# Feed-forward gate and up: high weights times both parts of x as one matmul of 512 columns, the halves added on the way out of PSUM

## The chip, the cores and the metric

The kernel runs on one core of one Trainium2 chip. The metric is the device time of one execution in microseconds; the median over the runs shown is used. Engines are named as in the profile: PE (TensorE's matmuls) and PEld (its weight loads), DVE (VectorE), ACT (ScalarE), POOL (GpSimd), SP (SyncE, which issues the DMAs).

## What is computed

A stack of four layers on one sequence of 256 tokens with 1024 features, in float32: two mixers with adaptive norms (sparse attention, dilated attention), and then two layers that each have a mixer (latent with sliding-window attention; forgetting with chunked attention) and a feed-forward part, each closed by a layer norm. The change touches the two feed-forward parts:

```python
def _swiglu(x, w_gate, w_up, w_down):
    g = jnp.einsum('bsd,df->bsf', x, w_gate)
    u = jnp.einsum('bsd,df->bsf', x, w_up)
    return jnp.einsum('bsf,fd->bsd', jax.nn.silu(g) * u, w_down)

    for layer in range(DEPTH):
        ...
        x = _layer_norm(DEEPNORM_ALPHA * x + mix, ln1_g[layer], ln1_b[layer])
        ffn = _swiglu(x, w_gate, w_up, w_down)
        x = _layer_norm(DEEPNORM_ALPHA * x + ffn, ln2_g[layer], ln2_b[layer])
```

Gate and up are 1024 x 2816, down is 2816 x 1024.

## The kernel before

Every float32 matrix product is made of three products of a narrower type (float32r). An operand is split exactly into a high part (rounded on ACT) and a low part (the rest, subtracted on DVE), and high x high, high x low and low x high are added up in PSUM. For activations `to_T` does this: four transposes on PE, a cast on ACT (L292), a subtraction on DVE (L293). The transposed operands of all 256 tokens stand in two tiles, `xh` and `xl`, of 8 chunks of 128 features by 256 tokens; `xt_tiles` gives the strips of 128 tokens of one block.

Weights are streamed in the order of use as units of 1024 floats per partition (512 KB). `make` loads a unit by DMA (L205), casts it on ACT (L210) and subtracts on DVE (L211). At most `NB` = 8 units stand ready or in use; `get` takes units, and `done`, called as the last products that use a unit are issued, lets the next one be made (`pump`). The new unit's cast waits until the slot that it takes over has been read.

`dense_T` computes 512 columns of x @ W, transposed: columns on the partitions, all 256 tokens along the free axis. It takes 4 units. For each pair of blocks of 128 columns it fills one PSUM bank, block after block, 256 floats each: 8 chunks of three products of 256 columns (L277 high weights with xh, L278 high weights with xl, L279 low weights with xh). Then the pair's sink is called. `dense_cols` is the other form, tokens on the partitions.

The feed-forward part (`ffn`) goes over the hidden features in six groups, the first of 256 columns (with `dense_cols`), five of 512 (with `dense_T`). For each group it computes gate, then up, then the products of the group before it with the down weights (`down`, L239, L240, L243 through `products`, 512 columns each). `gate_sink` makes a tanh on ACT (L472) and a product on DVE (L473); `up_sink` multiplies on DVE (L1035) and splits the hidden features by a cast on ACT (L1039) and a subtraction on DVE (L1040). PSUM banks go round by kind: four for the sums of `down`, three (4, 5, 6) of kind `gu` for gate and up, one for transposes.

The order of each engine's queue is fixed before the run by a scheduler that goes by dependences between parts of tiles, by its own model of time, and by priority; a sink stands 300 instructions ahead of its place in the program (`first(SINK)`). It is not written out by hand, so any edit may shift it.

Of the kernel before, what the change touches and what calls it, by code (L numbers as in the profile page):

```python
# [21 lines left out]
# priority, in instructions, that work of a kind has over what was emitted before it  # L22
SINK, HEAD, ATTN = 300, 60, 1200
# weights: floats of a unit per partition, units loaded ahead, units split ahead
UNIT, RAW, NB = 1024, 5, 8
# eighths of adaLN's rows loaded ahead
# [68 lines left out]
def body(ctx: ExitStack, tc: tile.TileContext, A: dict, out: bass.AP, stop=None):  # L95
# [17 lines left out]
    # ---- PSUM banks: each kind of tile goes round its own banks  # L113
# [12 lines left out]
    # ---- constants  # L126
# [52 lines left out]
    # ---- weights: streamed in order, split exactly into two float32r parts  # L179
# [6 lines left out]
    def spec(W, k0, nk, cols):  # L186
        """nk chunks of 128 rows of W from chunk k0 on, of the given ranges of columns side by side"""
        specs.append((W, k0, nk, cols))
# [42 lines left out]
    def products(p, terms, c, start=True, stop=True, after=None):  # L231
        """p += the products of chunks (xt, k) with (weights, kw): of the high parts of several chunks
        with both parts of the weights first, as the low parts come last"""
        n = len(terms)
        for t0 in range(0, n, state["group"]):
            group = range(t0, min(t0 + state["group"], n))
            for t in group:
                xt, k, w, kw = terms[t]
                pe.matmul(p, lhsT=xt[0][:, k, :], rhs=w[0][:, kw, c], start=start and t == 0, stop=False)  # L239
                pe.matmul(p, lhsT=xt[0][:, k, :], rhs=w[1][:, kw, c], start=False, stop=False)  # L240
            for t in group:
                xt, k, w, kw = terms[t]
                pe.matmul(p, lhsT=xt[1][:, k, :], rhs=w[0][:, kw, c], start=False, stop=stop and t == n - 1)  # L243
                if after is not None:
                    after(t)

    def dense_cols(xts, nk, n, sink, kind="mm"):
        """a group of n columns of x @ W, block of tokens after block of tokens; the sink takes them from PSUM"""
        step = UNIT // n
        units = -(-nk // step)  # L250
        ws = get(units)
        for tok in range(2):
            p = ps(kind)[:, :n]
            products(p, [(xts[tok], k, ws[k // step], k % step) for k in range(nk)], slice(0, n),
                     after=lambda k: tok and (k % step == step - 1 or k == nk - 1) and done(1))
            with first(SINK):
                sink(tok, p)

    # ---- transposed operands
    xh = ap_.tile([128, 8, 256], F32R, name="xh")  # L260
    xl = ap_.tile([128, 8, 256], F32R, name="xl")

    def xt_tiles(tok):
        """the operands of a block of tokens: one after the other they go over the same memory"""
        return tuple(t[:, :, tok * 128:(tok + 1) * 128] for t in (xh, xl))

    def dense_T(n, sink, kind="mm"):
        """n columns of x @ W, transposed: two blocks of 128 columns after the other, of all tokens"""
        ws = get(4)
        for pair in range(n // 256):  # L270
            p = ps(kind)
            for c in range(2):
                cols = slice(pair * 256 + c * 128, pair * 256 + c * 128 + 128)
                o = p[:, c * 256:(c + 1) * 256]
                for k in range(8):
                    w = [part[:, k % 2, cols] for part in ws[k // 2]]
                    pe.matmul(o, lhsT=w[0], rhs=xh[:, k, :], start=k == 0, stop=False)  # L277
                    pe.matmul(o, lhsT=w[0], rhs=xl[:, k, :], start=False, stop=False)  # L278
                    pe.matmul(o, lhsT=w[1], rhs=xh[:, k, :], start=False, stop=k == 7)  # L279
                    if pair == n // 256 - 1 and c and k % 2:  # L280
                        done(1)
            with first(SINK):
                sink(pair, p)

    def to_T(src, n, xt, k0):
        """n blocks of 128 columns, transposed and split, to chunks k0.. of xt"""
# [9 lines left out]
    def transposes(dst, srcs, eng, width=128):  # L296
        """up to four [128, width] blocks, transposed to dst [width, n, 128]"""
# [12 lines left out]
    # ---- norms  # L310
# [14 lines left out]
    def deepnorm(layer, which, last=False):  # L325
        """the sink of a product that closes a sublayer: x <- LN(alpha x + p) * g + b, and its transposed parts"""
# [28 lines left out]
    def gated(tok, h, p, g, tp):  # L355
        """x += p * g"""
# [16 lines left out]
    def project_out(xts, sink, order):  # L373
        """the products of the four chunks that come first, and then those of the others, that close a block of
        tokens before the next, so that a norm runs beside products; none but those of the norms' operands
        are split beside the last"""
# [14 lines left out]
    # ---- rotations  # L391
# [3 lines left out]
    def rope(dst, src, H, hd, cos, sin, tp):  # L395
        """dst = rotated src; src [128, H, 2*hd], dst the same or with copies side by side"""
# [13 lines left out]
    # ---- attention of a head: scores of both blocks of queries side by side, [128 | 256 keys]  # L410
    BLOCKS = ((0, 128), (128, 384))

    def scores(qT, kT, masks=None):
        """masks(tok): (lhsT, rhs, c0, c1) added on the tensor engine"""
# [8 lines left out]
    def shifted(s, added, n2, tp, scale=1.0):  # L423
        """-scale * (s + added), and its least value of each block of queries"""
# [11 lines left out]
    def av(e, v, o, c0, start, eng, tp, stop=True):  # L436
        """o[tok][:, c0:c0+64] += e of the block times v(block of keys)"""
# [12 lines left out]
    # of the keys of both blocks for the second block's queries; the first block's are the last 128  # L450
# [9 lines left out]
    def close_heads(o, den, oxt, k0, tp):  # L460
        """eight heads' sums over their denominators, transposed"""
# [7 lines left out]
    def silu2(p, dst, tp):  # L469
        """dst = 2 silu(p)"""  # L470
# [4 lines left out]
    # ---- the order of the weights  # L475
# [45 lines left out]
    # ---- adaLN  # L521
# [9 lines left out]
    def ada_rows(rows, new, ahead):  # L531
        """rows (name, layer, column): 1024 columns of silu(c) @ w + b on every partition;
        that of the scale: (1 + that) * the norm's gain. Returns the function that does the next eighth
        of a row, behind an instruction, and loads what is wanted some steps on"""
# [46 lines left out]
    # =====================================================================  # L581
    # layer 0: native sparse attention
# [17 lines left out]
    # the first columns of the mixer, chunk by chunk of the features, as adaLN gives them  # L600
# [64 lines left out]
    # nothing before the loads that the products wait for  # L665
# [11 lines left out]
    # the operands of the compression: [2 tokens of a block, features] by 16 pairs of tokens  # L677
# [4 lines left out]
    with first(ATTN):  # L682
        pool.tensor_copy(cmask, cc[:, C_CADD:C_CADD + 2 * NCMP].rearrange("p (t n) -> p t n", t=2))
        for tok in range(2):
# [6 lines left out]
            # the lower half one token on  # L691
# [14 lines left out]
    def k_side(p, tok, a, b, i):  # L706
        """rotated keys of both groups, twice side by side, transposed"""
# [13 lines left out]
    with first(SINK):  # L721
# [9 lines left out]
        # with the half that the gated z, twice a silu, asks for  # L731
# [23 lines left out]
    # keys: those of a group twice, block-diagonal, for a pair of heads at once  # L755
# [9 lines left out]
    # values: block-diagonal over the eight heads of a group  # L765
# [14 lines left out]
    def cmp_probs(tok, g):  # L780
# [11 lines left out]
        if tok == 0:  # L792
            # the first queries see no compressed key at all
# [16 lines left out]
    def nsa_head(g, hh, o):  # L810
        """selected blocks (all that there are) and window: both causal over all keys"""
# [77 lines left out]
    # =====================================================================  # L889
    # layer 1: dilated attention  # L890
    assign(mm=[0, 1], s=[2, 3], pt=[4, 5], o=[6, 7])
    with tc.tile_pool(name="dil", bufs=1) as dp:
# [42 lines left out]
        with first(ATTN):  # L935
# [4 lines left out]
            # the patterns' weights: softmax of logsumexp - log(heads), with 3 for the patterns  # L940
            # and the half that the gated z asks for; the gates of the second heads with all their factors
# [50 lines left out]
    # =====================================================================  # L992
    def ffn(layer, xt, last):
        state["group"] = 2
        assign(d=[0, 1, 2, 3], gu=[4, 5, 6], pt=[7])
        with tc.tile_pool(name=f"ffn{layer}", bufs=1) as fp:
# [3 lines left out]
            def down(parts, sink=None):  # L1000
                """parts of the hidden features into the sums, block of tokens after block of tokens"""
# [19 lines left out]
            for g, (a, b) in enumerate(ffn_groups):  # L1021
# [4 lines left out]

                def gate_sink(i, p):
                    m = p.shape[1]
# [3 lines left out]
                def up_sink(i, p):  # L1032
                    m = p.shape[1]
# [8 lines left out]
                if g:  # L1042
                    dense_T(n, gate_sink, "gu")
                    dense_T(n, up_sink, "gu")
# [14 lines left out]
    # =====================================================================  # L1059
    # layer 2: latent attention + sliding window  # L1060
    assign(mm=[0, 1], s=[2, 3], pt=[4, 5], o=[6, 7])
    state["group"] = 1
    with tc.tile_pool(name="ab", bufs=1) as bp:
# [30 lines left out]
        def qs_sink(pair, p):  # L1094
            # over the slopes, that come back with the distances
# [73 lines left out]
    # =====================================================================  # L1169
    # layer 3: forgetting attention + chunked attention with relative positions  # L1170
    assign(mm=[0, 1], s=[2, 3], pt=[4, 5], o=[6, 7])
    state["group"] = 1
    with tc.tile_pool(name="cd", bufs=1) as dp:
# [7 lines left out]
        # queries and keys with two more features that add the decays: (q, 1, cum q) . (k, -cum k, 1)  # L1181
# [17 lines left out]
        def fvf_sink(tok, p):  # L1199
            act.activation(fv[:, tok, 256:512], p[:, :256], AF.Copy)  # L1200
            # min(f, 0) - log(1 + exp(-|f|))
# [30 lines left out]
        with first(ATTN):  # L1232
# [8 lines left out]
            for h in range(8):  # L1241
                hs = slice((h % 2) * 64, (h % 2) * 64 + 64)
                # rel[q - k + 63] for the second block's queries, keys in reverse; the first block's are its last 128
# [23 lines left out]
def arrange(inputs):  # L1267
# [10 lines left out]
    # by head, and led by the 64 distances that the mask covers  # L1278
# [20 lines left out]
```

## Time and profile before

| | |
|---|---|
| runs (us) | 1024.37, 1039.41, 1026.41 |
| median (us) | 1026.41 |
| profiled execution: span from first to last instruction (us) | 1024.7 |
| profiled execution: its own time | not given |
| PE busy (us) | 978.7 |
| DVE busy (us) | 662.3 |
| ACT busy (us) | 508.4 |
| mean granted clock of TensorE | 0.980 |
| moved by DMA | 177.75 MB |

The profile is of one execution. Busy time of an engine is the union of its instructions. Matmuls are pipelined, so durations of neighbours overlap, and the pace is read from the starts. In brackets behind an instruction stand the idle time of its engine just before it and what ended that.

### The profile page before, as it was taken

Reading aid. Unit: us, or ns where it says so; the run is one execution under the profiler, and the core shown is the slowest. Engines: PE = TensorE matmul, PEld = TensorE weight load, DVE = VectorE, ACT = ScalarE, POOL = GpSimd, SP = SyncE. Lnnn points to the kernel's source line nnn. Section 1 sums busy time; section 2 is a strip of 40 time slices with the busy share of each in tenths; the row PEclk is TensorE's granted clock in tenths of the full one; section 3 lists DMA queues with packets and bytes.
Section 4 is the critical chain, followed back from the end, with each engine's and each line's share of the span. In section 5 each row is a group of like instructions: output and inputs, shape, how many; then the busy total and the mean of one; then the engine's idle time right before and its main releaser. Section 6 shows DMA issues by size and latency. Waiting matters only on the chain.

```text
span 1024.7 us, 16049 instructions
## 1 busy us (share of the span) xinstructions
PE 978.7 (96%) x6068; PEld 852.1 (83%) x6068; DVE 662.3 (65%) x1304; ACT 508.4 (50%) x967; POOL 39.0 (4%) x41
## 2 busy tenths in 40 slices
PE   5988999999999999999999999999999999999997
PEld 5877687777777878978899999978997789999995
DVE  5888788848776678665855555476454495544554
ACT  5584566734545536584343443335664344433440
POOL 1002000001220001000000000000000000000000
PEclk9998898999999999999999999999999999999999
DMA  9995776434865335632356455556543335455441
GB/s 287 309 308 182 249 241 201 129 101 134 261 191 179 119 102 190 229 103 64 99 208 205 165 194 206 176 171 190 170 145 99 112 117 192 165 202 189 165 144 42
DMA packets 106173, 177.75 MB, mean 173 GB/s; under 512 B 8816, under 2 KB 40688, under 8 KB 106096
## 3 DMA queue, kind: packets, MB, share of 16 engines
q1 hardware_dynamic: 106096, 176.72, 53.5%
q8 instruction: 48, 0.79, 0.3%
q14 instruction: 29, 0.24, 0.1%
HBM read 175.65 MB, written 1.05 MB: 172 GB/s over the span
## 4 chain that ended last, share of the span: by engine, by line
PE 83%; DVE 8%; DMA 4%; ACT 3%; issue 1%; SPq 0%; DVEq 0%; POOL 0%; ACTq 0%; POOLq 0%
PE ps L239 13%; PE ps L240 13%; PE ps L243 13%; PE ps L277 9%; PE ps L278 9%; PE ps L279 9%; PE ps L417 6%; PE ps L440 2%; DMA wr<-in_ada_w_dram 2%; PE ps L446 2%; DVE wl L211 2%; PE ps L447 2%; PE ps L448 2%; PE ps L289 1%; PE ps L300 1%
## 5 line engine op out<-in xcount | busy, mean ns | idle before, releaser
L211 DVE TENSOR_TENSOR wl<-wr,wh 128x1024 fp32r<-128x1024 f32 (+5 forms) x276 | 322.9, 1204 | 155.1 <-ACT wh L210 153.9
L210 ACT ACTIVATE wh<-wr 128x1024 fp32r<-128x1024 f32 (+5 forms) x276 | 270.5, 1022 | 168.2 <-PE ps L243 74.8
L277 PE MATMUL ps<-xh,wh 128*128 128x256 f32 x736 | 209.1, 284 | 0.0
L279 PE MATMUL ps<-xh,wl 128*128 128x256 f32 x736 | 208.9, 284 | 0.0
L278 PE MATMUL ps<-xl,wh 128*128 128x256 f32 x736 | 208.5, 283 | 0.0
L240 PE MATMUL ps<-wl,xh 128*128 128x512 f32 (+5 forms) x544 | 201.3, 373 | 0.4 <-DVE wl L211 0.4
L239 PE MATMUL ps<-wh,xh 128*128 128x512 f32 (+5 forms) x544 | 197.8, 376 | 3.9 <-ACT xh L292 2.6
L243 PE MATMUL ps<-wh,xl 128*128 128x512 f32 (+5 forms) x544 | 173.4, 372 | 1.0 <-DVE xl L293 0.8
L277 PEld LDWEIGHTS ps<-xh,wh 128*128 128x128 f32 x736 | 141.1, 192 | 0.5
L278 PEld LDWEIGHTS ps<-xl,wh 128*128 128x128 f32 x736 | 141.1, 192 | 0.3
L279 PEld LDWEIGHTS ps<-xh,wl 128*128 128x128 f32 x736 | 141.1, 192 | 0.1
L239 PEld LDWEIGHTS ps<-wh,xh 128*128 128x128 f32 x544 | 104.3, 193 | 22.7 <-ACT xh L292 6.2
L240 PEld LDWEIGHTS ps<-wl,xh 128*128 128x128 f32 x544 | 105.7, 194 | 16.1 <-issue 1.2
L243 PEld LDWEIGHTS ps<-wh,xl 128*128 128x128 f32 x544 | 101.1, 192 | 18.4 <-DVE xl L293 2.9
L239 PE MATMUL ps<-wh,hh 128*128 128x512 f32 x176 | 68.6, 390 | 0.0
L240 PE MATMUL ps<-wl,hh 128*128 128x512 f32 x176 | 68.6, 390 | 0.0
L243 PE MATMUL ps<-wh,hl 128*128 128x512 f32 x176 | 68.5, 389 | 0.0
L433 ACT ACTIVATE e<-e,sm 128x128 f32<-128x128 f32 x112 | 49.7, 446 | 19.7 <-DVE sm L427 19.5
L427 DVE CUSTOM_DVE_ANT_0 e<-ps,mask 128x128 f32<-128x128 f32 (+1 forms) x144 | 45.2, 352 | 20.4 <-PE ps L417 11.4
L292 ACT ACTIVATE xh<-ps 128x512 fp32r<-128x512 f32 x36 | 20.9, 597 | 75.0 <-PE ps L289 74.7
L314 POOL TENSOR_TENSOR sm<-sm,nhalf 128x1 f32<-128x1 f32 x18 | 12.7, 706 | 856.0 <-DVE sm L313 856.0
L564 DVE SCALAR_TENSOR_TENSOR ac<-ar,cs,ac 128x512 f32<-128x512 f32 x56 | 41.7, 745 | 1.0 <-DMA ar<-in_ada_w_dram 0.7
(319 smaller groups left out, 1230.8 us busy)
## 6 DMA issues: line engine op xcount, KB each, us to landing
wr<-in_ffn_w_gate_dram SPq DMA_DIRECT2D x44, 512.0 KB, 4.7
wr<-in_ffn_w_up_dram SPq DMA_DIRECT2D x44, 512.0 KB, 4.7
wr<-in_ffn_w_down_dram SPq DMA_DIRECT2D x44, 512.0 KB, 4.7
ar<-in_ada_w_dram SPq DMA_DIRECT2D x32, 512.0 KB, 4.5
wr<-in_dil_w_in_dram SPq DMA_DIRECT2D x32, 512.0 KB, 4.5
wr<-in_cd_w_in_dram SPq DMA_DIRECT2D x22, 512.0 KB, 4.7
wr<-in_ada_w_dram SPq DMA_DIRECT2D x32, 256.0 KB, 5.1
wr<-in_nsa_w_in_dram SPq DMA_DIRECT2D x12, 512.0 KB, 5.5
```

The source lines that it names most:

```text
L210: act.activation(hi, raw[:, :nk * n], AF.Copy)
L211: dve.tensor_sub(lo, raw[:, :nk * n], hi.bitcast(F32))
L239: pe.matmul(p, lhsT=xt[0][:, k, :], rhs=w[0][:, kw, c], start=start and t == 0, stop=False)
L240: pe.matmul(p, lhsT=xt[0][:, k, :], rhs=w[1][:, kw, c], start=False, stop=False)
L243: pe.matmul(p, lhsT=xt[1][:, k, :], rhs=w[0][:, kw, c], start=False, stop=stop and t == n - 1)
L277: pe.matmul(o, lhsT=w[0], rhs=xh[:, k, :], start=k == 0, stop=False)
L278: pe.matmul(o, lhsT=w[0], rhs=xl[:, k, :], start=False, stop=False)
L279: pe.matmul(o, lhsT=w[1], rhs=xh[:, k, :], start=False, stop=k == 7)
L417: pe.matmul(p[:, c0:c1], lhsT=qT(tok), rhs=kT[:, :c1 - c0], start=True, stop=masks is None)
L427: state["dve"] = dve.tensor_tensor_reduce(out=e[:, c0:c1], in0=s[:, c0:c1], in1=added[:, 256 - (c1 - c0):], scale=-scale, scalar=3e38, op0 ...
L433: act.activation(e[:, c0:c1], e[:, c0:c1], AF.Exp, bias=n2[:, i:i + 1], scale=-1.0, accum_out=den[:, i:i + 1])
L564: dve.scalar_tensor_tensor(ac, raw[:, j, :], cs[:, k:k + 1], ac, op0=ALU.mult, op1=ALU.add)
```

## The change

`xh` and `xl` become the halves of one tile, so that a chunk's high and low parts lie side by side, 512 floats. A new `dense_T2` takes the place of `dense_T` in groups 1 to 5 of the feed-forward parts (the other calls of `dense_T` stay). It gives each block of 128 columns a bank of its own: one product of the high weights with 512 columns (xh and xl), and one of the low weights with xh, added onto the first 256. The sink gets both banks of the pair, and `summed` adds their halves: a copy of the right half on ACT, an addition of the left half on DVE, each 128x256, into an SBUF tile that the sinks then read instead of PSUM. Comments and docstrings are taken out as well.

```diff
-    xh = ap_.tile([128, 8, 256], F32R, name="xh")
-    xl = ap_.tile([128, 8, 256], F32R, name="xl")
+    xhl = ap_.tile([128, 8, 2, 256], F32R, name="xhl")
+    xh, xl = xhl[:, :, 0], xhl[:, :, 1]
...
+    def dense_T2(n, sink, kind="mm"):
+        ws = get(4)
+        for pair in range(n // 256):
+            both = []
+            for c in range(2):
+                cols = slice(pair * 256 + c * 128, pair * 256 + c * 128 + 128)
+                p = ps(kind)
+                for k in range(8):
+                    w = [part[:, k % 2, cols] for part in ws[k // 2]]
+                    pe.matmul(p, lhsT=w[0], rhs=xhl[:, k].rearrange("p a t -> p (a t)"), start=k == 0, stop=False)
+                    pe.matmul(p[:, :256], lhsT=w[1], rhs=xh[:, k, :], start=False, stop=k == 7)
+                    if pair == n // 256 - 1 and c and k % 2:
+                        done(1)
+                both.append(p)
+            with first(SINK):
+                sink(pair, both)
...
+                def summed(both):
+                    t = fp.tile([128, 2, 256], F32, tag="hs", bufs=3, name=nm("hs"))
+                    for c, p in enumerate(both):
+                        act.activation(t[:, c], p[:, 256:], AF.Copy)
+                        dve.tensor_add(t[:, c], p[:, :256], t[:, c])
+                    return t.rearrange("p c t -> p (c t)")
+
                 def gate_sink(i, p):
+                    if g:
+                        p = summed(p)
                     m = p.shape[1]
...
                 def up_sink(i, p):
+                    if g:
+                        p = summed(p)
                     m = p.shape[1]
...
                 if g:
-                    dense_T(n, gate_sink, "gu")
-                    dense_T(n, up_sink, "gu")
+                    dense_T2(n, gate_sink, "gu")
+                    dense_T2(n, up_sink, "gu")
```

## Rows read from the trace of the kernel before

**Rows 1.** The page: busy times, DMA rate by slice, chain by engine and line.

```profile
PE 978.7 (96%) x6068; PEld 852.1 (83%) x6068; DVE 662.3 (65%) x1304; ACT 508.4 (50%) x967; POOL 39.0 (4%) x41
...
GB/s 287 309 308 182 249 241 201 129 101 134 261 191 179 119 102 190 229 103 64 99 208 205 165 194 206 176 171 190 170 145 99 112 117 192 165 202 189 165 144 42
...
PE 83%; DVE 8%; DMA 4%; ACT 3%; issue 1%; SPq 0%; DVEq 0%; POOL 0%; ACTq 0%; POOLq 0%
PE ps L239 13%; PE ps L240 13%; PE ps L243 13%; PE ps L277 9%; PE ps L278 9%; PE ps L279 9%; PE ps L417 6%; PE ps L440 2%; DMA wr<-in_ada_w_dram 2%; PE ps L446 2%; DVE wl L211 2%; PE ps L447 2%; PE ps L448 2%; PE ps L289 1%; PE ps L300 1%
```

**Rows 2.** Windows (one group, both stages): length; busy PE, PEld, DVE, ACT, POOL; clock; DMA; GB/s.

```profile
582.58:616.52 33.94, 33.94 (x243) 32.04 (x242) 17.76 (x18) 14.06 (x17) 0.00 (x0) 1.00 0.54 183
...
510.00:687.00 177.00, 177.00 (x1251) 166.99 (x1250) 98.27 (x107) 72.95 (x85) 0.92 (x1) 1.00 0.58 196
838.00:1014.00 176.00, 176.00 (x1246) 166.11 (x1245) 92.72 (x101) 68.70 (x80) 0.31 (x1) 1.00 0.50 169
```

**Rows 3.** Groups by line and shape, TensorE: busy us, mean ns.

```profile
L277 PE MATMUL ps<-xh,wh 128*128 128x256 f32 x736 | 209.1, 284 | 0.0
...
L239 PE MATMUL ps<-wh,hh 128*128 128x512 f32 x176 | 68.6, 390 | 0.0
```

**Rows 4.** Timeline of TensorE, from `down` to the next group's gate.

```profile
539.68 0.39 PE L243 MATMUL ps<-wh,hl 128*128 128x512 f32 x1
...
542.40 0.39 PE L243 MATMUL ps<-wh,hl 128*128 128x512 f32 x1
542.63 0.28 PE L277 MATMUL ps<-xh,wh 128*128 128x256 f32 x1
...
547.90 0.28 PE L279 MATMUL ps<-xh,wl 128*128 128x256 f32 x1
```

**Rows 5.** ACT and DVE at 128x256 (timeline); DVE at 128x512 (by shape: busy, mean ns).

```profile
516.52 0.39 ACT L292 ACTIVATE hh<-ps 128x256 fp32r<-128x256 f32 x1 [0.43 <-PE ps L289]
...
517.42 0.42 DVE L293 TENSOR_TENSOR hl<-ps,hh 128x256 fp32r<-128x256 f32 x1
...
L293 DVE TENSOR_TENSOR xl<-ps,xh 128x512 fp32r<-128x512 f32 x36 | 24.2, 686 | 23.9 <-ACT xh L292 23.9
...
L346 DVE SCALAR_TENSOR_TENSOR x<-x,sm,lg 128x512 f32<-128x512 f32 x16 | 11.2, 744 | 0.0
...
L335 DVE SCALAR_TENSOR_TENSOR x<-x,ps 128x512 f32<-128x512 f32 x16 | 10.9, 682 | 19.5 <-PE ps L243 19.5
```

**Rows 6.** Timeline of one steady group's gate: PE, ACT, DVE.

```profile
576.57 0.28 PE L277 MATMUL ps<-xh,wh 128*128 128x256 f32 x1
...
582.58 0.60 ACT L472 ACTIVATE th<-ps 128x512 f32<-128x512 f32 x1 [3.90 <-PE ps L279]
586.05 3.90 ACT L210 ACTIVATE wh<-wr 128x1024 fp32r<-128x1024 f32 x4 [2.87 <-PE ps L278]
589.86 0.58 ACT L472 ACTIVATE th<-ps 128x512 f32<-128x512 f32 x1
594.76 0.63 ACT L1039 ACTIVATE hh<-ht 128x512 fp32r<-128x512 f32 x1 [4.33 <-DVE ht L1035]
...
587.14 4.63 DVE L211 TENSOR_TENSOR wl<-wr,wh 128x1024 fp32r<-128x1024 f32 x4 [3.24 <-ACT wh L210]
591.69 0.68 DVE L473 SCALAR_TENSOR_TENSOR sg<-th,ps 128x512 f32<-128x512 f32 x1
594.04 0.69 DVE L1035 SCALAR_TENSOR_TENSOR ht<-sg,ps 128x512 f32<-128x512 f32 x1 [1.67 <-PE ps L279]
```

**Rows 7.** Waits of TensorE: us in total, times, longest.

```profile
PE ps L239 <- ACT xh L292: 2.6, 6, 0.7
...
PE ps L243 <- DVE xl L293: 0.8, 3, 0.3
```

**Rows 8.** Timeline where the first feed-forward stage opens: PE, DVE.

```profile
500.09 0.51 PE L243 MATMUL ps<-wh,xl 128*128 128x256 f32 x2 [0.30 <-DVE xl L293]
...
504.95 1.36 DVE L293 TENSOR_TENSOR xl<-ps,xh 128x512 fp32r<-128x512 f32 x2 [0.44 <-ACT xh L292]
```

## The prediction

> **What bounds the kernel now.** I read the page's busy times first, then its chain, then each feed-forward stage by windows, then single instructions. TensorE is busy 978.7 of 1024.7 us, and 83% of the chain that ended last is TensorE, 27% of it on the three lines of `dense_T` (L277 to L279) [rows 1]. In the windows the reader is to see that both feed-forward stages have TensorE busy for the whole stretch at a granted clock of 1.00, its upper level of 2.4 GHz, while DVE is busy for 98.3 of 177.0 us and ACT for 73.0 [rows 2]. One steady group of 512 hidden columns takes 33.94 us, all of it TensorE; DVE works 17.76 us of it, ACT 14.06, and the DMA moves 183 GB/s where the page has slices of over 300 [rows 1, 2]. So inside these stages only the pace of the products counts, and the rest matters if it comes late.
>
> The pace must not be read from an instruction's duration: products of 256 columns last 284 ns and those of 512 last 390 [rows 3], but they overlap. Starts tell it. Twelve 512-column steps take from 539.68 to 542.40, so b = 2.72 / 12 = 226.7 ns; 44 steps of 256 columns take from 542.63 to 547.90, so a = 5.27 / 44 = 119.8 ns [rows 4]. Check: a group has 4 blocks of columns x 2 (gate, up) x 24 = 192 products of 256 and 4 x 4 x 3 = 48 of 512, and 192 x 0.1198 + 48 x 0.2267 = 33.9 us, the window's length [rows 2]. The difference b - a = 106.9 ns is 256 columns at 2.4 GHz; so 119.8 - 106.9 = 12.9 ns of each product do not depend on its width.
>
> **The change, part by part.**
>
> *Products.* For each chunk and each block of 128 columns, L277 and L278 (same weights, xh then xl) become one product of 512 columns; that with the low weights stays at 256. Groups 1 to 5 of two layers have 2 x 5 x 2 x 4 x 8 = 640 such pairs; the other 96 of the 736 on L277 [rows 3] belong to three calls of `dense_T` that stay. The columns streamed are the same: one pair costs 2a = 239.6 ns before and b = 226.7 after, so 12.9 ns are saved, and 640 x 12.9 ns = 8.26 us. All of it lies on the path, as TensorE never pauses there. No row has a 512 and a 256 that take turns at every step, only the step from the one to the other at 542.40 to 542.63, 0.23 us, no longer than b [rows 4]. The bounds: nothing saved (the pair still costs 2a), or 12.9 ns; beyond that only if the weight load too were now better hidden, for which the 512 stream at b speaks no word. I take 12.9, the row nearest in shape. A weight load of 128 columns goes with each product, 640 fewer in all; they run beside the products.
>
> The Trainium skill (TensorE: Matmul & The Clock Gate, "Back-to-back issue gap") gives the gap as the columns over 2.4 GHz plus about 2.5 ns. By it a merge would save 2.5 ns, 1.6 us in all as an estimate. The trace has 12.9 in a stream with a weight load for every product, so it disagrees, and its number is used above.
>
> *The way out.* Per pair of blocks two ACT copies of 128x256 out of PSUM and two DVE additions of 128x256 with one operand in PSUM. Both operations have a row: 0.39 us for ACT, 0.42 for DVE [rows 5]. A group has 4 sinks, so 8 of each: ACT +3.1, DVE +3.4 us. The tanh and the two products on DVE now read SBUF instead of PSUM: the nearest DVE rows are 682 ns with PSUM and 744 with SBUF only [rows 5], so +0.06 us x 4. DVE comes to 17.76 + 3.4 + 0.2 = 21.4 of 33.1 us, ACT to 14.06 + 3.1 = 17.2. Over 10 groups that is 36 us of DVE and 31 of ACT, all beside products; I cost it at nothing. If the cover were gone, it would cost at each sink the copy, the addition and what is queued ahead of them. That is the question of the banks.
>
> *Banks.* A pair took one of the three banks of kind gu; now each block takes one. A block lasts 8 x (226.7 + 119.8) = 2.77 us, so a bank is wanted again 5.54 us after its last product. It is free after 0.26 us of latency (the steady tanh starts at 582.58, the pair's 48 products from 576.57 end at 582.32), copy and addition: 1.1 us if both engines are idle, which leaves 4.4 us for queues. They are idle after the first pair of gate (ACT had waited 3.90 us at 582.58) and of up (DVE 1.67 us at 594.04) [rows 6]. The bad place is the second pair of gate: its last block frees four weight units, and four casts of 3.90 us in a row start at 586.05 on ACT, four subtractions of 4.63 us at 587.14 on DVE. The pair ends at 588.07, the tanh comes at 589.86, 1.8 us late, and the sg of DVE at 591.69 [rows 6]. If order stays so, the copy of the second block ends 2.2 us after the pair, its addition, behind the subtractions, 591.77 + 0.42 - 588.07 = 4.1 us after it. Allowed are 5.54; 1.4 us to spare. The first block has been done for 2.77 us by then, and its copy depends on its own bank alone, before the first cast has its slot; I expect it there. So no new wait of TensorE.
>
> *What else is moved.* No DMA is added; the units are asked for at the same points, 0.83 us per group earlier. The same megabytes in 33.1 instead of 33.9 us ask for 188 GB/s. The last group's sum is wanted after another `down` of 48 x 0.2267 = 10.9 us; the longer chain of its sink (about 1.6 us) hides there. xh and xl become parts of one tile; if reads and writes of the two were kept apart less finely, product starts would wait for xl.
>
> **The sum.** The profiled span is 1024.7 us; 1024.7 - 8.3 = 1016.4. The median of the three runs, 1026.41, is 1.7 above that span (the lowest, 1024.37, 0.3 below it; the profiled execution's own time is not given), so I forecast 1016.4 + 1.7 = 1018 us.
>
> **Rivals.**
>
> *A. The pair saves nothing.* The 12.9 ns could come with each 256 columns moved or with each change of shape and not with each instruction; then the mixed stream costs 3a per step as before. For it: no row shows the mix. Against it: a product of 512 has the 12.9 ns once, not twice [rows 4]. Time: 1026; by half the gain, 1022. The page named above makes the gain small too.
>
> *B. The banks turn too slowly, and it is slower.* If both copies of the second gate pair are queued behind the four casts, and the additions behind the subtractions, then the first block's bank is free 4.1 us after the pair and wanted at 2.77: TensorE stands 1.35 us, once in a group, 10 x 1.35 = 13.5 us, net 5.2 slower: 1031.6. It decides from 0.83 us per group (8.26 / 10); for over 2% slower it would take (20.5 + 8.3) / 10 = 2.9 us per group, that is, more pairs held than this one. For it: the tanh was put behind the casts in every steady group. Against it: that tanh waited for the second block, the first copy does not.
>
> *C. The one tile for xh and xl ties them together.* Then products with the high parts would wait for the low ones, 0.69 us later, at up to the 36 writes of xl in the kernel [rows 5]: at most 24.7 us, 1043. Such waits are seldom last now: 2.6 us on xh, 0.8 on xl [rows 7]. Against it: the two blocks of tokens are interleaved in one tile already, and products of the first (500.09) run before the second's strips are written (504.95), though they come later in the program [rows 8].
>
> **How the numbers follow.** Forecast (6 to 11 us saved) 0.66; A 0.13, B 0.13, C 0.04; 0.04 for other shifts, as the order of every queue is made anew. Below, another order may give a few us: 1013. Above, the range takes in A and reaches just short of B: 1030. About 2%, 20.5 us, is what a measurement here can tell from no change: faster by that needs 12 us that no step has, 0.02; slower, B with several pairs or all of C, 0.05; within, 0.93.
>
> **What would show it.** Right: starts of products in gate and up alternate by 0.23 and 0.12 us, a group takes 33.1 us, TensorE stays fully busy in both stages, ACT copies of the first block come before the casts. Wrong: a group above 33.9 us; a wait of TensorE for the new addition (B), or at the openings of sublayers for xl (C); steps of 0.24 us (A).

## The result, and the profile after

The changed kernel takes 1018.83 us (median of 6 runs, 1015.48 to 1020.13), the kernel before 1025.39 in the same comparison (6 runs). The ratio is 0.994 with a 95% interval of 0.9915 to 0.9966, so 3.5 to 8.7 us were gained. The forecast was 1018 us, a gain of 8.3. The sections below show that the two feed-forward stages account for about half of that forecast. Ratios, here and below, are taken from each kernel's faster runs; left out are, among others, one run of the kernel with two banks (3288.73 us) and one of that with four (1032.12 us).

The page of the changed kernel, as in [rows 1] (busy times; L279 is now the wide product, L280 the narrow one):

```profile
PE 968.1 (95%) x5428; PEld 812.5 (80%) x5428; DVE 695.0 (68%) x1384; ACT 538.4 (53%) x1047; POOL 38.8 (4%) x41
```

TensorE has lost 640 instructions and 10.6 us of busy time; DVE has gained 32.7 us (662.3 to 695.0) and ACT 30.0 (508.4 to 538.4). The windows, columns as in [rows 2]: the first feed-forward stage from the first product of group 1 to the first transpose of the closing norm, and one steady group.

```profile
510.89:684.27 173.38, 173.38 (x910) 147.96 (x909) 113.48 (x146) 86.49 (x122) 0.92 (x1) 1.00 0.55 192
579.58:613.09 33.51, 33.51 (x179) 28.63 (x178) 21.09 (x26) 17.08 (x25) 0.00 (x0) 1.00 0.55 188
```

The same stage of the kernel before, cut at the same two instructions:

```profile
513.70:689.27 175.57, 175.57 (x1230) 165.11 (x1229) 96.84 (x106) 71.30 (x82) 0.92 (x1) 1.00 0.56 190
```

The second stage of both kernels, before and then after, from the first product of group 1 (after: from the two transposes ahead of it, which stand inside the stage elsewhere) to the start of the last product of `down`:

```profile
841.37:1016.71 175.34, 175.34 (x1229) 164.99 (x1228) 92.06 (x101) 67.30 (x78) 0.92 (x1) 1.00 0.48 163
```

```profile
834.39:1007.43 173.04, 173.04 (x910) 147.80 (x908) 107.84 (x141) 80.90 (x118) 0.92 (x1) 1.00 0.47 163
```

The reader is to see that TensorE is busy for the whole of both stages in both kernels, at the upper level of its clock, that the first stage went from 175.57 to 173.38 us, 2.19 less, and the second from 175.34 to 173.04, 2.30 less. The steady group went from 33.94 us [rows 2] to 33.51: 0.43 us, where the forecast had 0.83. The added work, by line (busy us, mean ns; behind the bar the idle time ahead of it):

```profile
L279 PE MATMUL ps<-xhl,wh 128*128 128x512 f32 x640 | 226.6, 398 | 0.0
L280 PE MATMUL ps<-xhl,wl 128*128 128x256 f32 x640 | 179.4, 281 | 0.0
...
L1052 DVE TENSOR_TENSOR hs<-ps,hs 128x256 f32<-128x256 f32 x80 | 32.8, 421 | 68.2 <-ACT hs L1051 68.1
...
L1051 ACT ACTIVATE hs<-ps 128x256 f32<-128x256 f32 x80 | 30.2, 379 | 98.3 <-PE ps L280 98.2
```

The copy measured 379 ns and the addition 421, as their nearest rows had it (0.39 and 0.42 us) [rows 5]. The pace of the products, from the starts as in [rows 4]:

```profile
606.37 0.39 PE L279 MATMUL ps<-xhl,wh 128*128 128x512 f32 x1
606.60 0.28 PE L280 MATMUL ps<-xhl,wl 128*128 128x256 f32 x1
606.71 0.40 PE L279 MATMUL ps<-xhl,wh 128*128 128x512 f32 x1
606.95 0.28 PE L280 MATMUL ps<-xhl,wl 128*128 128x256 f32 x1
...
623.33 0.40 PE L239 MATMUL ps<-wh,hh 128*128 128x512 f32 x1
```

Between 606.37 and the first product of `down` at 623.33 there are 6 blocks of 8 pairs: 16.96 / 48 = 353.3 ns a pair. The uniform paces, taken from longer stretches than in the prediction, are 23.03 / 192 = 119.95 ns for 256 columns and 10.91 / 48 = 227.3 for 512 (gate and up, and then `down`, of a steady group of before, which opens at 576.57 [rows 6]):

```profile
599.60 0.40 PE L239 MATMUL ps<-wh,hh 128*128 128x512 f32 x1
...
610.51 0.28 PE L277 MATMUL ps<-xh,wh 128*128 128x256 f32 x1
```

Three narrow ones cost 359.9 ns; one wide and one narrow should cost 347.2. The pair saves 6.6 ns and not 12.7. Note how the starts lie: 0.23 or 0.24 us after a wide product, 0.11 or 0.12 after a narrow one, so that no single step looks wrong. Only the sum over many does.

### The profile page after: what moved, and what is told of

It reads as the page before. It is cut to its first block, busy times and chain, and to the rows that moved or that the text cites. A ratio compares the mean times of both kernels' runs of the same rounds, so it can differ in the third digit from the quotient of the medians.

```text
span 1015.4 us, 14901 instructions
## 1 busy us (share of the span) xinstructions
PE 968.1 (95%) x5428; PEld 812.5 (80%) x5428; DVE 695.0 (68%) x1384; ACT 538.4 (53%) x1047; POOL 38.8 (4%) x41
## 4 chain that ended last, share of the span: by engine, by line
PE 81%; DVE 8%; DMA 5%; ACT 3%; issue 2%; SPq 1%; POOL 0%; DVEq 0%; ACTq 0%; POOLq 0%
PE ps L279 15%; PE ps L239 13%; PE ps L240 12%; PE ps L243 12%; PE ps L280 7%; PE ps L437 6%; PE ps L460 2%; DMA wr<-in_ada_w_dram 2%; DVE wl L211 2%; DMA wr<-in_nsa_w_in_dram 2%; PE ps L466 1%; PE ps L467 1%; PE ps L468 1%; ACT wh L210 1%; PE ps L309 1%
## 5 line engine op out<-in xcount | busy, mean ns | idle before, releaser
L279 PE MATMUL ps<-xhl,wh 128*128 128x512 f32 x640 | 226.6, 398 | 0.0
L239 PE MATMUL ps<-wh,xhl 128*128 128x512 f32 (+5 forms) x544 | 196.7, 374 | 4.5 <-ACT xhl L312 2.5
L240 PE MATMUL ps<-wl,xhl 128*128 128x512 f32 (+5 forms) x544 | 198.9, 369 | 0.1
L280 PE MATMUL ps<-xhl,wl 128*128 128x256 f32 x640 | 179.4, 281 | 0.0
L243 PE MATMUL ps<-wh,xhl 128*128 128x512 f32 (+5 forms) x544 | 172.0, 369 | 1.0 <-DVE xhl L313 0.8
L279 PEld LDWEIGHTS ps<-xhl,wh 128*128 128x128 f32 x640 | 120.0, 188 | 28.9
L239 PEld LDWEIGHTS ps<-wh,xhl 128*128 128x128 f32 x544 | 103.3, 191 | 23.9 <-ACT xhl L312 6.4
L280 PEld LDWEIGHTS ps<-xhl,wl 128*128 128x128 f32 x640 | 120.9, 189 | 1.0
L240 PEld LDWEIGHTS ps<-wl,xhl 128*128 128x128 f32 x544 | 104.0, 191 | 15.4 <-issue 1.2
L243 PEld LDWEIGHTS ps<-wh,xhl 128*128 128x128 f32 x544 | 100.3, 191 | 18.1 <-DVE xhl L313 2.9
L1051 ACT ACTIVATE hs<-ps 128x256 f32<-128x256 f32 x80 | 30.2, 379 | 98.3 <-PE ps L280 98.2
L1052 DVE TENSOR_TENSOR hs<-ps,hs 128x256 f32<-128x256 f32 x80 | 32.8, 421 | 68.2 <-ACT hs L1051 68.1
L334 POOL TENSOR_TENSOR sm<-sm,nhalf 128x1 f32<-128x1 f32 x18 | 12.7, 707 | 846.4 <-DVE sm L333 846.4
```

The costliest lines, as they stand in the source:

```text
L279: pe.matmul(p, lhsT=w[0], rhs=xhl[:, k].rearrange("p a t -> p (a t)"), start=k == 0, stop=False)
L280: pe.matmul(p[:, :256], lhsT=w[1], rhs=xh[:, k, :], start=False, stop=k == 7)
L1052: dve.tensor_add(t[:, c], p[:, :256], t[:, c])
```

## The experiments

The first four kernels share the runs of the kernel before (median 1024.29, 35 runs). For the others there are 13 runs of it each (median 1025.10 for two banks, 1024.12 for four). The five kernels in the sections on weights, bank, width and neighbours ran once each, and only the pace in their traces is read.

### One part of the change alone: the tile, and the way out

The kernel before with only the operand tile of the change:

```diff
-    xh = ap_.tile([128, 8, 256], F32R, name="xh")
-    xl = ap_.tile([128, 8, 256], F32R, name="xl")
+    xhl = ap_.tile([128, 8, 2, 256], F32R, name="xhl")
+    xh, xl = xhl[:, :, 0], xhl[:, :, 1]
```

Expected: 

> The kernel before with only the operand tile of the change (xh and xl as the halves of one tile); products and sinks as before. Theory (the tile does nothing to the time): ratio 1.000, a group 33.94 us, TensorE's waits for xh and xl as before, 2.6 and 0.8 us. Rival (parts of one tile tie each other): waits for xl in place of those for xh, up to 25 us more; or, if the layout itself gave the part of the gain that the steps don't explain, a ratio of 0.996 to 0.998.

Measured: ratio 0.9992 (0.9971 to 1.0014). The stage by windows, and TensorE's groups by line that waited for xh and xl (idle time behind the bar, now under the name xhl):

```profile
514.22:689.79 175.57, 175.57 (x1231) 165.11 (x1229) 96.92 (x106) 71.18 (x82) 0.92 (x1) 1.00 0.56 191
```

```profile
L239 PE MATMUL ps<-wh,xhl 128*128 128x512 f32 (+5 forms) x544 | 196.4, 374 | 4.0 <-ACT xhl L292 2.7 <-ACT xhl L644 0.8
L243 PE MATMUL ps<-wh,xhl 128*128 128x512 f32 (+5 forms) x544 | 172.8, 371 | 1.0 <-DVE xhl L293 0.8
```

The stage is that of before to the hundredth, 175.57 us, and the waits are 2.7 us for the high parts and 0.8 for the low, against 2.6 and 0.8 [rows 7]. The tile alone does nothing, and rival C falls. The changed kernel shows the same:

```profile
PE ps L239 <- ACT xhl L312: 2.5, 6, 0.7
...
PE ps L243 <- DVE xhl L313: 0.8, 3, 0.3
```

The other part alone is the changed kernel with its wide product taken apart again:

```diff
-                    pe.matmul(p, lhsT=w[0], rhs=xhl[:, k].rearrange("p a t -> p (a t)"), start=k == 0, stop=False)
+                    pe.matmul(p[:, :256], lhsT=w[0], rhs=xh[:, k, :], start=k == 0, stop=False)
+                    pe.matmul(p[:, 256:], lhsT=w[0], rhs=xl[:, k, :], start=False, stop=False)
```

Expected: 

> The changed kernel with the wide product taken apart again: for each chunk three products of 256 columns, a bank a block, the halves added by ACT and DVE. Theory (the way out is hidden by the products): three steps of 119.8 ns, 33.94 us a group, no wait of TensorE for the additions, ratio 0.998 to 1.002. Rival (copies and additions hold banks or weights): a group longer than 33.94 us, ratio above 1.003.

Measured: ratio 0.9997 (0.9971 to 1.0023), and the stage:

```profile
510.20:685.88 175.68, 175.68 (x1231) 165.12 (x1230) 113.20 (x146) 86.30 (x122) 0.92 (x1) 1.00 0.55 190
```

175.68 us with DVE at 113.2 us instead of 96.8: 16 us more of DVE, 15 of ACT, and 0.11 us of the stage. The way out is hidden. What the change gains comes from the wide product alone.

### Why a pair costs 353 ns: the order of the widths

Two orders of the same products, with 8 and with 2 for STEP:

```diff
-                for k in range(8):
-                    w = [part[:, k % 2, cols] for part in ws[k // 2]]
-                    pe.matmul(p, lhsT=w[0], rhs=xhl[:, k].rearrange("p a t -> p (a t)"), start=k == 0, stop=False)
-                    pe.matmul(p[:, :256], lhsT=w[1], rhs=xh[:, k, :], start=False, stop=k == 7)
+                for k0 in range(0, 8, STEP):
+                    for k in range(k0, k0 + STEP):
+                        w = ws[k // 2][0][:, k % 2, cols]
+                        pe.matmul(p, lhsT=w, rhs=xhl[:, k].rearrange("p a t -> p (a t)"), start=k == 0, stop=False)
+                    for k in range(k0, k0 + STEP):
+                        w = ws[k // 2][1][:, k % 2, cols]
+                        pe.matmul(p[:, :256], lhsT=w, rhs=xh[:, k, :], start=False, stop=k == 7)
```

Expected of eight and eight: 

> Change of order only: in each block of 128 columns the eight products of 512 columns come first, then the eight of 256. Theory (the step from wide to narrow and back costs): eight and eight keep the pace of the two uniform streams of before, 8 x (226.7 + 119.8) = 2.77 us a block instead of the 2.82 us (16.95 us / 6) seen when they take turns; a steady group takes 33.1 us instead of 33.51, the kernel about 4 us less than the changed one, ratio to before near 0.990. Rival (a product with xh and xl side by side costs 6.8 ns more wherever it stands): 2.82 us a block, 33.5 us a group, the changed kernel's time.

Measured: ratio 0.9926 (0.9899 to 0.9953), 1017.74 us. The gate and the first pair of up take from 605.71 to 622.44, 16.73 / 48 = 348.5 ns a pair (x8 merges eight products):

```profile
605.71 1.98 PE L280 MATMUL ps<-xhl,wh 128*128 128x512 f32 x8
...
622.44 0.40 PE L239 MATMUL ps<-wh,hh 128*128 128x512 f32 x1
```

The stage:

```profile
511.02:683.04 172.02, 172.02 (x910) 148.28 (x909) 113.40 (x146) 86.44 (x122) 0.92 (x1) 1.00 0.56 193
```

Expected of two and two: 

> Change of order only: two products of 512 columns, then two of 256, four times a block. Theory (each change of width costs): half the changes, so half of the extra time, 2.80 us a block and 33.3 us a group. Rival (the wide product itself costs more): 2.82 us and 33.5 us.

Measured: ratio 0.9948 (0.9919 to 0.9978), 1017.32 us. Timeline of TensorE (x2 merges two products), and the stage by windows:

```profile
609.14 0.62 PE L280 MATMUL ps<-xhl,wh 128*128 128x512 f32 x2
609.60 0.40 PE L283 MATMUL ps<-xhl,wl 128*128 128x256 f32 x2
...
625.85 0.40 PE L239 MATMUL ps<-wh,hh 128*128 128x512 f32 x1
```

```profile
514.58:686.38 171.80, 171.80 (x911) 147.19 (x910) 113.21 (x146) 86.33 (x122) 0.92 (x1) 1.00 0.56 193
```

From 609.14 to 625.85 it is 16.71 / 48 = 348.1 ns a pair. So the theory was right that the order costs, and wrong in its form: I had expected the extra to go with the number of changes of width, and two and two, with four times as many changes as eight and eight, is not slower (stage 171.80 against 172.02). The rival, that the wide product itself costs more, falls: the same products run 5 ns a pair faster. Both orders save 1.4 to 1.6 us in the first stage over the change, so 2 to 3 us in all; by their ratios they can't be told from it, as the intervals overlap, but their runs lie about 2 us lower at the same granted clock (see "The total" below). Eight and eight, too, stays above the uniform sum, by 1.3 ns a pair or 10 ns a block.

### What of the alternation costs: weights, bank or width

First the pace with the high weights in both products of a pair:

```diff
-                    pe.matmul(p[:, :256], lhsT=w[1], rhs=xh[:, k, :], start=False, stop=k == 7)
+                    pe.matmul(p[:, :256], lhsT=w[0], rhs=xh[:, k, :], start=False, stop=k == 7)
```

Expected: 

> The changed kernel with the high weights in the narrow product too (the low part of the weights is left out of gate and up): widths still take turns 512, 256, 512, 256, but every product of a chunk loads the same tile. Theory W (one wide and one narrow in turn cost it, whatever the weights): 353 ns a pair, 16.95 us for the 48 pairs before the first part of the down products. Theory L (the turn between the tiles of high and low weights costs it): 346 to 348 ns a pair, 16.65 to 16.7 us.

Measured, TensorE's first wide product of gate and the first of `down` behind 48 pairs:

```profile
608.47 0.39 PE L279 MATMUL ps<-xhl,wh 128*128 128x512 f32 x1
...
625.42 0.40 PE L239 MATMUL ps<-wh,hh 128*128 128x512 f32 x1
```

16.95 us: 353.1 ns, as in the changed kernel. The turn between the two weight tiles is not it.

The narrow product added onto the right half of the bank, `p[:, 256:]` for `p[:, :256]`:

Expected: 

> The changed kernel with the narrow product added onto the right half of the bank instead of the left (the sum of the halves is the same). Theory W and theory L: no difference, 16.95 us for 48 pairs, 33.5 us a group. Rival P (the step back in the bank, from column 511 to 0, or the wait for a column written shortly before costs it): another pace, below 16.9 or above 17.0.

```profile
612.16 0.39 PE L279 MATMUL ps<-xhl,wh 128*128 128x512 f32 x1
...
629.11 0.40 PE L239 MATMUL ps<-wh,hh 128*128 128x512 f32 x1
```

16.95 us again, so it isn't the columns of the bank either.

Widths all 256, weights in turn:

```diff
-                    pe.matmul(p, lhsT=w[0], rhs=xhl[:, k].rearrange("p a t -> p (a t)"), start=k == 0, stop=False)
-                    pe.matmul(p[:, :256], lhsT=w[1], rhs=xh[:, k, :], start=False, stop=k == 7)
+                    pe.matmul(p[:, :256], lhsT=w[0], rhs=xh[:, k, :], start=k == 0, stop=False)
+                    pe.matmul(p[:, 256:], lhsT=w[1], rhs=xh[:, k, :], start=False, stop=k == 7)
```

Expected: 

> Products of one width, 256 columns, with high and low weights in turn (for each chunk high weights x xh on the left half, low weights x xh on the right; the product of the high weights with xl is left out of gate and up). Theory W: the uniform pace, 119.8 ns each, 239.6 ns for the two, 11.50 us for 96. Theory L: as much more as in the changed kernel, 246 ns for the two, 11.8 us.

```profile
562.56 0.28 PE L279 MATMUL ps<-xhl,wh 128*128 128x256 f32 x1
...
574.07 0.40 PE L239 MATMUL ps<-wh,hh 128*128 128x512 f32 x1
```

96 products in 11.51 us, 119.9 ns each: the uniform pace. Of the three suspects the width in turn is left.

### Which neighbour costs: a single narrow or a single wide product

For every other chunk one product is left out, so that the widths come as 512, 512, 256 (the first) or 512, 256, 256 (the second):

```diff
-                    pe.matmul(p[:, :256], lhsT=w[1], rhs=xh[:, k, :], start=False, stop=k == 7)
+                    if k % 2:
+                        pe.matmul(p[:, :256], lhsT=w[1], rhs=xh[:, k, :], start=False, stop=k == 7)
...
-                    pe.matmul(p, lhsT=w[0], rhs=xhl[:, k].rearrange("p a t -> p (a t)"), start=k == 0, stop=False)
+                    if k % 2 == 0:
+                        pe.matmul(p, lhsT=w[0], rhs=xhl[:, k].rearrange("p a t -> p (a t)"), start=k == 0, stop=False)
```

Expected of two wide, one narrow: 

> Widths 512, 512, 256 in turn (the product with the low weights is left out for every other chunk of gate and up). The uniform paces of before are 227.3 and 119.95 ns, so three steps come to 574.6 ns, a block of four such rounds to 2.298 us and six blocks to 13.79 us. Theory N (a single narrow product between wide ones costs the extra 6 ns, as it stood in the changed kernel and did not in the order two and two): 580.5 ns, six blocks 13.93 us. Theory D (a single wide product between narrow ones costs it): 13.79 us.

```profile
595.41 0.62 PE L279 MATMUL ps<-xhl,wh 128*128 128x512 f32 x2
595.86 0.28 PE L281 MATMUL ps<-xhl,wl 128*128 128x256 f32 x1
...
609.46 0.39 PE L239 MATMUL ps<-wh,hh 128*128 128x512 f32 x1
```

The 24 rounds from 595.41 to 609.46 are 14.05 us, 585.4 ns a round where uniform paces give 574.6: 10.8 ns more for each single narrow product.

Expected of one wide, two narrow: 

> Widths 512, 256, 256 in turn (the product of the high weights with both parts of x is left out for every other chunk of gate and up). Uniform paces: 467.2 ns for three, a block 1.869 us, six blocks 11.21 us where TensorE has no wait. Theory N: 11.21 us. Theory D: 473 ns, six blocks 11.36 us. If both runs show the extra, either single product costs it.

```profile
862.00 0.40 PE L280 MATMUL ps<-xhl,wh 128*128 128x512 f32 x1
862.23 0.40 PE L281 MATMUL ps<-xhl,wl 128*128 128x256 f32 x2
...
870.40 0.86 PE L239 MATMUL ps<-wh,hh 128*128 128x512 f32 x3
```

The 18 rounds from 862.00 to 870.40, in the second stage, are 466.7 ns each; the uniform sum is 467.2. (Over six blocks this run can't be read, since TensorE waits for additions in some of them; all 284 rounds of the run that take less than 500 ns have a mean of 468.5.) So a wide product alone between narrow ones costs next to nothing, and a narrow one alone between wide ones costs 6 to 11 ns. Theory N holds in its place; its size was expected as 6 ns in both patterns and is 10.8 where two wide ones stand between. Nor is a lone narrow product the whole of it, as eight and eight has none and keeps 10 ns a block. Why is open. What the trace of the changed kernel shows beside it is that the weight load of a product starts with the product ahead of it (the load for the wide product of 606.71 starts at 606.60, with the narrow one), so that beside a narrow product stands the load for the wide one; that this is the cause was not tried.

### The banks

Two banks of kind gu instead of three, `gu=[4, 5]`:

Expected: 

> The changed kernel with two banks for gate and up instead of three. A block lasts 2.82 us, so each bank must be emptied within one block: 0.26 us, copy 0.39, addition 0.42 and what is queued ahead on ACT (four casts, 3.9 us) and DVE (four subtractions, 4.6 us). Theory (the third bank is what hides the way out): TensorE waits for additions, or the order of its queue is filled with more of the down products; where the queues hold a block by 4.1 us the wait is about 1.3 us, two or three times a group, 25 to 40 us over ten groups, ratio 1.02 to 1.04. Rival (two banks would do, since the scheduler puts down products in between): group within 0.3 us of 33.5, ratio within 0.99 to 1.00.

Measured: ratio 1.0087 (1.0057 to 1.0116), 1035.45 us. Windows of the whole stage, of a steady group and of the rest of the stage, and TensorE's waits:

```profile
508.42:693.42 185.00, 177.50 (x932) 150.44 (x931) 115.49 (x154) 86.66 (x123) 0.92 (x1) 0.99 0.54 185
642.35:676.28 33.93, 33.16 (x175) 28.04 (x174) 20.23 (x26) 16.20 (x25) 0.00 (x0) 1.00 0.50 177
676.28:693.42 17.14, 12.01 (x52) 9.30 (x50) 14.96 (x27) 4.45 (x5) 0.92 (x1) 0.94 0.73 255
```

```profile
PE ps L309 <- DVE x L367: 6.5, 3, 4.7
...
PE ps L279 <- DVE hs L1052: 4.8, 7, 1.1
```

The steady group is 0.42 us longer than in the changed kernel (33.93 against 33.51), and waits for the additions come to 4.8 us in the whole program, a fifth of the lower figure expected. The larger part lies at the end of the stage: of its last 17.14 us TensorE works 12.01, and the norm's transposes wait for x 6.5 us in all. The whole stage, from the first product of group 1, takes 185.00 us. In it stand 24 products of group 0 which run ahead of the stage with three banks, 24 x 0.12 = 2.9 us, so it is 8.7 us longer than with three. The granted clock falls as well: it is 0.94 in the last 17.14 us, where TensorE pauses, and 1.00 in the whole stage with three banks. What fits the pause is the order: with two banks the scheduler put more products of `down` between the blocks of up, and after the last block 61 are left where the changed kernel has 83, so fewer for the norm to hide behind; that this alone is the cause was not tried apart. The theory was right in sign and in that the third bank is needed, and wrong in place and size (it had 1.02 to 1.04).

Four banks, `gu=[4, 5, 6, 7]`:

Expected: 

> The changed kernel with four banks for gate and up (the fourth shared with the transposes). Theory (three banks already hide the way out on the chip; only the order is made for the model's wait): the products of down no longer stand in the middle of up, or fewer of them, a group still takes 33.5 us, ratio to before 0.991 to 0.997 as for the change. Rival (the bank wait costs something in the changed kernel): a group under 33.4 us.

Measured: ratio 0.9987 (0.9947 to 1.0028). That holds no change and overlaps the interval of the change, but lies above the 0.991 to 0.997 expected. The stage tells more:

```profile
512.88:686.27 173.39, 173.39 (x910) 147.92 (x909) 112.98 (x146) 85.79 (x122) 0.92 (x1) 1.00 0.56 191
```

173.39 us against 173.38, and at the same granted clock the runs lie where those of the change do ("The total"). In the changed kernel the trace has a dozen products of `down` between the first and second pair of up (from 623.33 to 626.28); with four banks they are gone in the steady groups, so they stand there for the bank that the scheduler's model awaits. On the chip neither costs anything.

## Why the prediction was right, and where it was not

**The bound.** Right. Both stages stay with TensorE busy throughout, DVE at 21.09 us and ACT at 17.08 of a group; forecast were 21.4 and 17.2.

**The products.** Right in kind, mis-sized in amount. The step that failed is the one where I took the pair's price as b, with 12.9 ns saved, as "the row nearest in shape". The row had one width only, and the mix is what the change runs: 6.6 ns are saved a pair. Over both stages that is 640 x 6.6 ns = 4.2 us, and the windows of the stages say nearly the same, 2.19 + 2.30 = 4.5, against the 8.26 forecast. The prediction had said that no row has the two widths in turn and kept both ends, 0 and 12.9; the truth lies in the middle, and "half the gain, 1022" of rival A names it. Rival A's reason, that a change of shape costs, came near: not each change alike, but most where a narrow product stands alone among wide ones. The Trainium skill (TensorE: Matmul & The Clock Gate, "Back-to-back issue gap") has a fixed 2.5 ns for a product, and calls this the gap of an isolated one, without weight loads, which the prediction did not say. In this stream, with a weight load for every product, 11.4 ns a pair are saved in the order eight and eight and 11.8 in two and two.

**The way out.** Right, and shown by itself: 0.11 us in the first stage. One small term was too high: the DVE operations that now read SBUF were put at +0.06 us by rows that also take a scalar per partition; L1067, without one, takes 692 ns where L1035 took 684. Another was left out: the tanh that now reads SBUF takes 632 ns on ACT where it took 588. Neither lies on the path.

**The banks.** Right that no wait comes, also in the detail. ACT and DVE in the gate of a steady group:

```profile
612.22 0.38 ACT L1051 ACTIVATE hs<-ps 128x256 f32<-128x256 f32 x1 [2.38 <-PE ps L280]
...
615.05 0.38 ACT L1051 ACTIVATE hs<-ps 128x256 f32<-128x256 f32 x1 [1.32 <-PE ps L280]
615.67 3.90 ACT L210 ACTIVATE wh<-wr 128x1024 fp32r<-128x1024 f32 x4 [0.24 <-PE ps L279]
619.49 0.36 ACT L1051 ACTIVATE hs<-ps 128x256 f32<-128x256 f32 x1
```

```profile
616.77 4.63 DVE L211 TENSOR_TENSOR wl<-wr,wh 128x1024 fp32r<-128x1024 f32 x4 [0.88 <-ACT wh L210]
621.32 0.75 DVE L1052 TENSOR_TENSOR hs<-ps,hs 128x256 f32<-128x256 f32 x2
```

The copy of the second pair's first block stands at 615.05, ahead of the four casts at 615.67, as forecast; that of the last block comes behind them, at 619.49, and its addition behind the four subtractions at 621.32. The block ended where up begins, at 617.66; its addition ends 621.74, 4.1 us later, the figure of the prediction. What I had not seen is that the scheduler, with its own model of this wait, would move products of `down` into up. It cost nothing here.

**The tile.** Right: nothing.

**The total.** That 1018 stands so near 1018.83 is luck, and so is it that the medians fall among the "6 to 11 us saved". The stages give 4.5 us where the forecast had 8.3; the medians differ by 6.6, inside an interval of 3.5 to 8.7. The profiled spans, 1024.7 and 1015.4, differ by 9.3, and 4.8 of that lies outside the two stages, where the change touches only the tile and the order of the queues. The two stretches ahead of the stages, before and then after:

```profile
0.00:513.70 513.70, 479.13 (x2679) 393.75 (x2679) 380.22 (x916) 288.37 (x652) 33.93 (x35) 0.97 0.59 184
689.27:841.37 152.10, 148.26 (x935) 128.28 (x934) 88.22 (x175) 81.39 (x156) 2.35 (x3) 0.98 0.42 131
```

```profile
0.00:510.89 510.89, 475.45 (x2678) 390.68 (x2679) 380.02 (x916) 288.77 (x653) 33.62 (x35) 0.98 0.58 186
684.27:834.39 150.12, 145.86 (x936) 126.09 (x934) 88.72 (x175) 82.23 (x156) 2.37 (x3) 1.00 0.43 136
```

The numbers of products are the same to one, and the granted clock differs: 0.97 and 0.98 before, 0.98 and 1.00 after. It differs as much between runs of one kernel. In the 61 runs of the kernel before that have their clock on record (35 and twice 13), it lies between 0.968 and 0.988, and the time follows a straight line in it, 7.8 us for each 0.01, with a scatter of 1.1 us around it. At the same granted clock the six runs of the changed kernel lie 4.3 us below this line (an estimate, standard error about 0.6), which is what the stages gave. By the same line the tile alone lies 0.5 us above and the way out alone 0.4, two and two lies 6.7 us below, eight and eight 6.5, four banks 3.8, and two banks lies 8.8 above (without its run of 3288.73 us).

The kernel with the right half of the bank shows the same. It has the queue orders of the changed kernel on every engine, and its span is 7 us longer at the same 16.95 us, with a clock of 0.978 where the changed kernel's profile has 0.988:

```profile
core 0: 1022.5 us, clock 0.978
```

So the profiled spans may not be subtracted; the stage's windows, all at a clock of 1.00, may.

## What to carry to other kernels

When two matmuls with the same stationary operand are merged into one of twice the width, what is saved is the fixed part of one instruction, here 6.6 to 11.8 ns, and not the 178 ns by which two durations of 284 exceed one of 390: read the pace from starts over dozens of instructions. If the merge leaves narrow products among wide ones, put the narrow ones two or more together: the changed kernel gave half of its gain back by taking turns one by one. Extra work on idle engines was free as long as each block's bank had two blocks' time (5.6 us) to be emptied; with one block's time it was not, and the loss appeared in another place, at the end of the stage. Small gains are compared in windows at one granted clock, or between runs of the same granted clock: 0.01 of it was worth 7.8 us here, more than the whole change.

## What the runs showed of the hardware that was not expected

A product of 256 columns alone between products of 512 makes the round about 6 ns (one wide, one narrow) or 10.8 ns (two wide, one narrow) longer than the uniform paces add up to; in the orders two and two and eight and eight about 1 ns a pair is added (348.1 and 348.5 against 347.2), and a wide one alone between pairs of narrow ones adds next to nothing (466.7 against 467.2). The weights and the half of the bank make no difference (16.95 us for 48 pairs with either, 16.96 in the changed kernel).
